# Dense attention scores as two 64-row matmuls, issued for two key blocks at a time

## The chip, the cores and the metric

The kernel runs on all 8 cores of one Trainium2 chip, two sequences of the batch on each core, with nothing exchanged between them. The metric is the device time of the slowest core, in microseconds (us). Some executions fall into a slower state in which the four cores of one die, sometimes of both, show a lower granted TensorE clock (0.816 on one die against 0.991 on the other in the changed kernel's run of 4770 us; 0.924 to 0.921 and 0.919 to 0.914 on both in one of 4394 us in experiment 6).

## The reference, cut to what matters

```python
x = x + 0.5 * swiglu(rmsnorm(x), gate1, up1, down1)
h = rmsnorm(x)
q_A, k_A, v_A, q_B, k_B, v_B, gates = split(h @ w_in)
# A: dense differential attention: 8 heads, each with two score maps (head dimension 64)
p = softmax(q_A @ k_A.T * 64**-0.5 - slope * |distance|)      # (head, 2, query, key)
o_A = rmsnorm((p[0] - lam * p[1]) @ v_A)                      # value dimension 128
# B: windowed attention: 16 heads of dimension 64, |distance| <= 128, with a sink
x = x + (sig(g_A) * (o_A @ P_A) + sig(g_B) * (o_B @ P_B)) @ w_out
x = x + 0.5 * swiglu(rmsnorm(x), gate2, up2, down2)
```

Both attentions contract over 64 elements for their scores, half of the 128 rows that TensorE's full matmuls have in the profile ("128*128"). The dense one has two score maps per head, so two contractions over 64 belong together.

## The kernel before: the parts that matter

The attention of a sequence is a list of steps. A dense step covers one block of 128 keys and a block of 384 (or 256) queries. It makes scores for both maps (QK) on TensorE (PE in the profile), takes exp on ScalarE (ACT), multiplies by a table of position biases on VectorE (DVE), and, LAG steps later, multiplies with the values (AV) on TensorE. When a block of queries is done, its AV sums are copied out of their PSUM banks, scaled, normalised and transposed in parts spread over the next steps; this is the evacuation. The two stretches of the run in which attention is at work, one for each sequence, are the attention phases. The steps are interleaved with matmuls of the feed-forward and projection stages ("fill"), so that TensorE has work while ACT and DVE are busy. A yielded number is a cost in TensorE columns, by which the fill is metered out.

```python
def attention(self, sq):
    # ... steps: per head 96 dense ("D"), then 16 windowed ("S")
    for i in range(n + LAG + 14):
        due = [f for (d, f) in self.later if d <= i]
        self.later = [x for x in self.later if x[0] > i]
        for f in due:
            yield f()                       # later parts of an evacuation
        if i < n:
            yield self.b_qk(i, steps[i])
        if LAG <= i < n + LAG:              # LAG = 3
            yield from self.b_av(i, steps[i - LAG], sq)

def b_qk(self, i, st):
    s = self.pslot()                        # one of two score slots, two PSUM banks each
    er, et = self.er[i % 2], self.et[i % NET]   # NET = 6
    # ...
    for c in range(2):
        ps = slice(64 * c, 64 * c + 64)
        if kind == "D":                     # kz[:, c] holds map c's keys, and zeros in the other half
            self.mm(self.bk[2 * s + c][:, 0:W], self.kz[:, c, k0:k0 + 128], self.q[0][:, q0:q0 + W], ...)
        else:                               # 64 rows of the array for each map
            self.mm(self.bk[2 * s + c][:, 0:W], self.k1[ps, k0:k0 + 128], self.q[1][ps, q0:q0 + W], ...)
    self.act(er[:, :, 0:W], <both banks of slot s>, AF.Exp, ..., scale=0.125)
    self.tt(et[:, :, 0:W], er[:, :, 0:W], tab, ALU.mult, ...)
    return 2 * W if kind == "D" else W + 400
```

A dense map's keys stand in one half of the rows with zeros in the other, so that the matmul has the full form (128*128 in the profile, 0.162 us from start to start at 384 columns) and there is no switch of tiling, which cost the windowed steps of before 0.094 us in and 0.103 us out. `load_D` loads a head's keys, queries, values and bias table when the head before has ended.

The softmax here doesn't subtract the row's maximum and nothing guards it: scores larger than these inputs give would overflow.

## Time and profile before

| | before |
|---|---|
| median of 5 runs, two of them slow | 4217.02 us (fast ones: 4207.8, 4216.3, 4217.0) |
| profiled run, slowest core | 4206.8 us |
| TensorE (PE) busy | 97% |
| attention phases, slowest core | 1170 and 1179 us |
| matmuls | 27872 in the program, the same number after |

Matmul durations in the profile overlap: a 512-column one is 382 ns long, but the next starts 216 ns after it. What counts is the distance from one start to the next, which a timeline gives. The prediction shows the lines.

### The profile page before, as it was taken

What the parts mean: (1) busy time and instruction counts of PE and PEld (TensorE: products, weight loads), DVE (VectorE), ACT (ScalarE), POOL (GpSimd) and SP (SyncE); (2) the same over time, 40 slices, a digit from 0 to 9 for tenths busy, and PEclk for the clock granted to TensorE, in tenths of its full rate; (3) what the DMA queues carried; (4) which work ended last, traced back from release to release, by engine and by line L of the source; (5) the groups of instructions that cost most, each with busy time, mean ns of one, the idle gap of its engine ahead of it and who ended that gap; (6) DMA issues with size and microseconds to landing.
All of it is one profiled execution on the core that took longest, in us unless ns stands there. A gap on an engine that the chain in (4) does not pass through costs nothing.

```text
span 4206.8 us, 82560 instructions; the slowest of 8 cores (4178.8 to 4206.8 us)
## 1 busy us (share of the span) xinstructions
PE 4084.3 (97%) x28032; PEld 2276.0 (54%) x28032; DVE 2319.0 (55%) x4768; ACT 2111.7 (50%) x3814; POOL 177.2 (4%) x235
## 2 busy tenths in 40 slices
PE   7999999999999999999999999999999999999998
PEld 3445445555665566556565565566556444444443
DVE  4332352447766765766357766776776544343533
ACT  2111421257777777777367777776777312121211
POOL 1000000000000000000000000000000000000000
PEclk9999999999999999999999999999999999999999
DMA  7977776656565655656944423443343465555543
GB/s 172 186 189 207 238 222 198 215 157 173 141 165 154 167 139 152 172 157 156 245 143 151 143 96 121 154 138 103 125 135 123 142 221 168 195 177 186 189 150 132
DMA packets 220581, 693.93 MB, mean 165 GB/s; under 512 B 22256, under 2 KB 80880, under 8 KB 218096
## 3 DMA queue, kind: packets, MB, share of 16 engines
q1 hardware_dynamic: 212432, 634.11, 47.6%
q0 software_dynamic: 7744, 54.53, 8.4%
q8 instruction: 240, 3.93, 0.4%
q14 instruction: 165, 1.35, 0.1%
HBM read 614.27 MB, written 160.79 MB: 184 GB/s over the span
## 4 chain that ended last, share of the span: by engine, by line
PE 85%; DMA 7%; DVE 3%; ACT 2%; issue 2%; SPq 1%; DVEq 0%; ACTq 0%; POOL 0%; POOLq 0%
PE bank L306 84%; DMA td<-td_d 2%; ACT er L309 1%; SPq L330 1%; DMA rd<-s_d 1%; DVE et L312 1%; DMA s_win<-ra 1%; DMA rd<-w_d 1%; DMA R<-x 1%; DMA vd_d<-sv 1%; PE bank L941 1%; DMA ra<-s_win 0%; DMA x_d<-R 0%; DMA qd_d<-sq 0%; DVE R L315 0%
## 5 line engine op out<-in xcount | busy, mean ns | idle before, releaser
L306 PE MATMUL bank<-H,ra 128*128 128x512 bf16 x8320 | 2200.8, 382 | 25.8 <-DMA ra<-s_win 6.1
L309 ACT ACTIVATE er<-bank 128x768 bf16<-128x768 f32 (+1 forms) x1792 | 1323.5, 745 | 571.5 <-PE bank L306 426.3
L306 PEld LDWEIGHTS bank<-H,ra 128*128 128x128 bf16 x8320 | 796.1, 99 | 772.5 <-issue 114.4
L312 DVE TENSOR_TENSOR et<-er,td 128x768 bf16<-128x768 bf16 (+1 forms) x1536 | 780.0, 512 | 637.3 <-ACT er L309 604.5
L306 PE MATMUL bank<-aT,rd 128*128 128x512 bf16 x2816 | 753.6, 382 | 15.2 <-DMA rd<-s_d 8.2
L306 PEld LDWEIGHTS bank<-vD,et 128*128 128x128 bf16 x8192 | 593.0, 98 | 286.0 <-issue 25.5
L306 PE MATMUL bank<-vD,et 128*128 128x129 bf16 x8192 | 723.2, 221 | 15.3 <-DVE obs L312 5.5
L306 PE MATMUL bank<-q,kz 128*128 128x384 bf16 (+1 forms) x3072 | 697.7, 309 | 10.7 <-ACT er L309 6.9
L315 DVE SCALAR_TENSOR_TENSOR fr<-fr,bank 128x512 f32<-128x512 f32 x480 | 329.4, 686 | 435.0 <-ACT fr L309 334.9
L309 ACT ACTIVATE fr<-bank 128x512 f32<-128x512 f32 x352 | 209.5, 595 | 665.0 <-PE bank L306 664.8
L306 PEld LDWEIGHTS bank<-q,kz 128*128 128x128 bf16 x3072 | 291.6, 98 | 261.3 <-issue 39.4
L306 PEld LDWEIGHTS bank<-aT,rd 128*128 128x128 bf16 x2816 | 267.4, 98 | 257.3 <-issue 40.1
L315 DVE SCALAR_TENSOR_TENSOR R<-bank,R 128x512 f32<-128x512 f32 x192 | 132.2, 688 | 301.1 <-PE bank L306 301.0
L312 DVE TENSOR_TENSOR aT<-fr,bank 128x512 bf16<-128x512 f32 x352 | 240.8, 684 | 71.3 <-PE bank L306 68.8
L309 ACT ACTIVATE fr<-bank,bgh 128x512 f32<-128x512 f32 x128 | 87.7, 686 | 291.3 <-PE bank L306 290.9
L309 ACT ACTIVATE ntmp<-R 128x512 f32<-128x512 f32 x224 | 135.5, 625 | 156.2 <-DVE R L315 109.0
L312 DVE TENSOR_TENSOR nacc<-nacc,ntmp 128x512 f32<-128x512 f32 x224 | 153.9, 687 | 62.1 <-ACT ntmp L309 59.9
L312 POOL TENSOR_TENSOR rs<-ms,mhalf 128x3 f32<-128x3 f32 (+1 forms) x96 | 88.1, 917 | 2181.9 <-DVE ms L321 2181.9
L312 DVE TENSOR_TENSOR et<-er,sw 128x768 bf16<-128x768 bf16 (+1 forms) x256 | 135.5, 538 | 65.8 <-ACT er L309 63.9
L306 PE MATMUL bank<-ra,H 128*128 128x256 bf16 x1280 | 169.3, 273 | 1.4 <-ACT sv L309 1.3
L327 DVE CAST sq<-bank 128x512 bf16<-128x512 f32 x104 | 71.5, 688 | 159.2 <-PE bank L306 113.7
L309 ACT ACTIVATE sq<-bank 128x512 bf16<-128x512 f32 x104 | 61.8, 596 | 187.4 <-PE bank L306 135.3
(84 smaller groups left out, 2360.5 us busy)
## 6 DMA issues: line engine op xcount, KB each, us to landing
ra<-s_gu SPq DMA_DIRECT2D x308, 512.0 KB, 4.4
rd<-s_d SPq DMA_DIRECT2D x112, 704.0 KB, 4.3
ra<-s_win SPq DMA_DIRECT2D x116, 512.0 KB, 5.7
ra<-s_pg SPq DMA_DIRECT2D x64, 512.0 KB, 3.7
ra<-s_pp SPq DMA_DIRECT2D x64, 512.0 KB, 3.4
R<-x SPq DMA_DIRECT2D x32, 512.0 KB, 7.8
x_d<-R SPq DMA_DIRECT2D x32, 512.0 KB, 6.2
R<-x_d SPq DMA_DIRECT2D x32, 512.0 KB, 6.6
```

What stands on the lines that cost most here:

```text
L306: self.S.add("pe", lambda e: e.matmul(out, lhsT=lhsT, rhs=rhs, start=start, stop=stop), r=r, w=w)
L309: self.S.add("act", lambda e: e.activation(out=out, in_=in_, func=func, **kw), r=r, w=w)
L312: self.S.add(eng, lambda e: e.tensor_tensor(out=out, in0=a, in1=b, op=op), r=r, w=w)
L315: self.S.add("dve", lambda e: e.scalar_tensor_tensor(out=out, in0=a, scalar=s, in1=b, op0=op0, op1=op1), r=r, w=w)
L327: self.S.add(eng, lambda e: e.tensor_copy(out=out, in_=in_), r=r, w=w)
L330: self.S.add(eng, lambda e: e.dma_start(out=out, in_=in_), r=r, w=w, dma=sem)
L941: self.S.add("pe", lambda e, q=q: e.transpose(out=bt[:, q * 128:(q + 1) * 128], in_=src[:, q, :], identity=self.ident), r=[sk, "ident"], w ...
```

## The change

Its intent is to make use of both halves of the array: the two maps' QK become two 64-row matmuls that run side by side, as the windowed ones of before do (starts 0.003 us apart in the median of its trace). As each switch of tiling costs time (0.094 us in and 0.103 us out, by the prediction's reading of the trace before), two steps are issued together, so that four matmuls share one entry and one exit. The windowed steps, tiled already, are paired too. The lag grows to 4 steps and there are more buffers. Queries and bias table are loaded in two parts, the first one earlier. Casting later weights to bf16 is tied to attention steps. The pacing constants are new. The later parts of an evacuation are now issued after a step's scores and AV, and no longer ahead of them. The core of the diff, with cuts marked:

```diff
-LAG = 3
-NET = 6
+QT = 14
+LAG = 4
+NET = 8
+QK2 = {384: 1375, 256: 1130}
...
-        self.kz = sb("kz", [128, 2, SEQ], BF16)
+        self.k0 = sb("k0", [128, SEQ], BF16)
...
-            if i < n:
-                yield self.b_qk(i, steps[i])
+            if i % 2 == 0 and i < n:
+                yield self.b_qk(i, steps[i:i + 2], sq)
...
+        for kind, u, bi, kc in sts:
...
+            s = self.pslot()
+            todo.append((s, W, tab, tk))
+            for c in range(2):
+                ps = slice(64 * c, 64 * c + 64)
+                self.mm(self.bk[2 * s + c][:, 0:W], k[ps, kc * 128:(kc + 1) * 128], q[ps, q0:q0 + W], True, True,
                         qk, [("bk", 2 * s + c)])
...
+        for n, (s, W, tab, tk) in enumerate(todo):
...  (exp and product of each step, as before)
+        if kind == "D" and bi == 5 and kc == 0 and u < 7:
+            self.load_D(sq, u + 1, 0, self.dma)
+        if kind == "D" and self.ahead and (bi < 4 and kc == 2 or bi == 2 and kc == 10):
+            self.precast(self.ahead.pop(0))
+        return QK2[W] + (720 if kind == "S" else 0)
...
-                    self.load_D(sq, u + 1, self.dma)
+                    self.load_D(sq, u + 1, 1, self.dma)
```

More of the change, by code (lines that the diff above doesn't have):

```diff
@@ L238, in decl_chip @@
         self.obf = sb("obf", [128, 3, 128], BF16)
-        self.obs = [sb("obs%d" % i, [128, 3, 128], BF16) for i in range(3)]
+        self.obs = [sb("obs%d" % i, [128, 3, 128], BF16) for i in range(4)]
         self.obn = 0
@@ L265, in decl_chip @@
         assert b0 + 39424 + NFF * TB * 2 <= self.ptr
-        self.ALIAS = (["q0", "q1", "k0a", "k0b", "kz", "k1", "k1b", "vD", "vS", "td0", "td1", "sw"] + ["er%d" % i for i in range(2)] +
+        self.ALIAS = (["q0a", "q0b", "q1", "k0", "k1", "k1b", "vD", "vS", "td0", "td1", "sw"] + ["er%d" % i for i in range(2)] +
                       ["et%d" % i for i in range(NET)])
@@ L278, in decl_chip @@
         self.drip = []
-        self.casting = False
     def bank(self, hold=False):
@@ L355, in init_rings @@
                       [("gu2", f) for f in range(22)] + [("d2", c) for c in range(8)])
-        self.nis = 0
     def issue(self, k, after=()):
@@ L361, in issue @@
             self.drip.pop(0)()
-        if self.ahead and self.casting:
-            self.nis += 1
-            if self.nis % 3 == 0:
-                self.precast(self.ahead.pop(0))
     def flush(self):
@@ L471, in setup2 @@
                 yield
-            if h == 7:
-                for j in range(2):
-                    S.add("dve", lambda e, j=j: e.memset(self.kz[64 - 64 * j:128 - 64 * j, j, :], 0.0), w=["kz", "dd"] + al)
             self.dma(self.td_d[h], self.tst[h % 2], [("tst", h % 2, j) for j in range(4)] + al, [("tdd", h)], ("c", 6 + h % 2))
@@ L653, in st_W @@
             if i == 8 and b % 4 == 3:
-                self.load_D(b // 4, 0, self.slow)
+                self.load_D(b // 4, 0, 0, self.slow)
+                self.load_D(b // 4, 0, 1, self.slow)
             if i == 1 and b == 7:
@@ L762, in st_O, with load_D @@
             self.issue("a")
-    def load_D(self, sq, h, dma):
-        c = slice(sq * SEQ, (sq + 1) * SEQ)
+    def load_D(self, sq, h, part, dma):
+        c0 = sq * SEQ
         bl = range(4 * sq, 4 * sq + 4)
-        for j in range(2):
-            dma(self.kz[64 * j:64 * j + 64, j, :], self.kd_d[h * 128 + 64 * j:h * 128 + 64 * j + 64, c],
-                [("kd", h // 2, b) for b in bl], ["k0" + "ab"[j]], ("bkz", j))
-        dma(self.q[0], self.qd_d[h * 128:(h + 1) * 128, c], [("qd", h // 2, b) for b in bl], ["q0"], ("bq", 0))
-        dma(self.vD, self.vd_d[sq, h], [("vd", sq, h // 2, b) for b in bl], ["vD"], ("bv", 0))
-        for j in range(2):
-            n = slice(NM // 2 * j, NM // 2 * (j + 1))
-            dma(self.td[:, n], self.td_d[h][:, n], [("tdd", h)], ["td%d" % j], ("btd", j))
+        n = slice(0, QT * 128) if part == 0 else slice(QT * 128, SEQ)
+        m = slice(0, QT * 128) if part == 0 else slice(QT * 128, NM)
+        r = slice(h * 128, (h + 1) * 128)
+        if part == 1:
+            dma(self.k0, self.kd_d[r, c0:c0 + SEQ], [("kd", h // 2, b) for b in bl], ["k0"], ("bk", 0))
+        dma(self.q[0][:, n], self.qd_d[r, c0 + n.start:c0 + n.stop], [("qd", h // 2, b) for b in bl],
+            ["q0" + "ab"[part]], ("bq0", part))
+        if part == 1:
+            dma(self.vD, self.vd_d[sq, h], [("vd", sq, h // 2, b) for b in bl], ["vD"], ("bv", 0))
+        dma(self.td[:, m], self.td_d[h][:, m], [("tdd", h)], ["td%d" % part], ("btd", part))
     def load_S(self, sq, p, dma):
@@ L797, in attention @@
         self.load_S(sq, 0, self.slow)
-        for i in range(n + LAG + 14):
-            due = [f for (d, f) in self.later if d <= i]
-            self.later = [x for x in self.later if x[0] > i]
-            for f in due:
-                yield f()
-            if i < n:
-                yield self.b_qk(i, steps[i])
+        for i in range(n + LAG + 15):
+            if i % 2 == 0 and i < n:
+                yield self.b_qk(i, steps[i:i + 2], sq)
             if LAG <= i < n + LAG:
                 yield from self.b_av(i, steps[i - LAG], sq)
+            for f in self.due(i):
+                yield f()
@@ L807, in attention @@
         assert not self.later
-    def b_qk(self, i, st):
-        kind, u, bi, kc = st
-        s = self.pslot()
-        er, et = self.er[i % 2], self.et[i % NET]
-        if kind == "D":
-            t0, nq = QBLOCKS[bi]
-            q0, W, sl = t0 * 128, nq * 128, 0
-            m0 = q0 - kc * 128 + 1920
-            tab = self.td[:, m0:m0 + W].unsqueeze(1).broadcast_to([128, 2, W])
-            tk, qk = ["td0", "td1"], ["q0", "k0a", "k0b", "kz"]
-        else:
-            lo, hi = max(0, kc - 1), min(15, kc + 1)
-            q0, W, sl = lo * 128, (hi - lo + 1) * 128, 1
-            off = (lo - kc + 1) * 128
-            tab = self.sw[:, :, off:off + W]
-            tk, qk = ["sw"], ["q1", "k1", "k1b"]
-        k0 = kc * 128
-        for c in range(2):
-            ps = slice(64 * c, 64 * c + 64)
-            if kind == "D":
-                self.mm(self.bk[2 * s + c][:, 0:W], self.kz[:, c, k0:k0 + 128], self.q[0][:, q0:q0 + W], True, True,
-                        qk, [("bk", 2 * s + c)])
-            else:
-                self.mm(self.bk[2 * s + c][:, 0:W], self.k1[ps, k0:k0 + 128], self.q[1][ps, q0:q0 + W], True, True,
-                        qk, [("bk", 2 * s + c)])
-        self.act(er[:, :, 0:W], self.ps[s].rearrange("p (c w) -> p c w", c=2)[:, :, 0:W], AF.Exp,
-                 [("bk", 2 * s), ("bk", 2 * s + 1)], ["er%d" % (i % 2)], scale=0.125)
-        self.tt(et[:, :, 0:W], er[:, :, 0:W], tab, ALU.mult, ["er%d" % (i % 2)] + tk, ["et%d" % (i % NET)])
-        return 2 * W if kind == "D" else W + 400
@@ new lines, in due, with b_qk @@
+    def due(self, i):
+        now = [f for (d, f) in self.later if d <= i]
+        self.later = [x for x in self.later if x[0] > i]
+        return now
+    def b_qk(self, i, sts, sq):
+        todo = []
+        for kind, u, bi, kc in sts:
+            if kind == "D":
+                t0, nq = QBLOCKS[bi]
+                q0, W = t0 * 128, nq * 128
+                m0 = q0 - kc * 128 + 1920
+                tab = self.td[:, m0:m0 + W].unsqueeze(1).broadcast_to([128, 2, W])
+                tk = ["td0"] * (m0 < QT * 128) + ["td1"] * (m0 + W > QT * 128)
+                q, k, qk = self.q[0], self.k0, ["q0a" if t0 < QT else "q0b", "k0"]
+            else:
+                lo, hi = max(0, kc - 1), min(15, kc + 1)
+                q0, W = lo * 128, (hi - lo + 1) * 128
+                off = (lo - kc + 1) * 128
+                tab = self.sw[:, :, off:off + W]
+                tk, q, k, qk = ["sw"], self.q[1], self.k1, ["q1", "k1", "k1b"]
+            s = self.pslot()
[3 more added lines that the diff above has]
+                self.mm(self.bk[2 * s + c][:, 0:W], k[ps, kc * 128:(kc + 1) * 128], q[ps, q0:q0 + W], True, True,
+                        qk, [("bk", 2 * s + c)])
+        for n, (s, W, tab, tk) in enumerate(todo):
+            x, y = (i + n) % 2, (i + n) % NET
+            er, et = self.er[x], self.et[y]
+            self.act(er[:, :, 0:W], self.ps[s].rearrange("p (c w) -> p c w", c=2)[:, :, 0:W], AF.Exp,
+                     [("bk", 2 * s), ("bk", 2 * s + 1)], ["er%d" % x], scale=0.125)
+            self.tt(et[:, :, 0:W], er[:, :, 0:W], tab, ALU.mult, ["er%d" % x] + tk, ["et%d" % y])
+        kind, u, bi, kc = sts[0]
+        if kind == "D" and bi == 5 and kc == 0 and u < 7:
[3 more added lines that the diff above has]
+        return QK2[W] + (720 if kind == "S" else 0)
@@ L920, in evac_D @@
         self.later += [(i + 1, f1), (i + 3, f1b), (i + 4, f2), (i + 6, f3), (i + 7, f3b), (i + 9, f4),
-                       (i + 13, lambda: self.tposes(self.obf, "obf", 0, t0, nq, self.od_d, "od", sq, u, bi == 5))]
+                       ((i + 14) & ~1, lambda: self.tposes(self.obf, "obf", 0, t0, nq, self.od_d, "od", sq, u, bi == 5))]
     def evac_S(self, i, sq, u, gi, bank):
@@ L925, in evac_S @@
         self.obn += 1
-        oi = self.obn % 3
+        oi = self.obn % 4
         obs, ok = self.obs[oi], ("obs", oi)
@@ L933, in evac_S @@
                 self.rn[:, 0:ng, :].unsqueeze(3).broadcast_to([128, ng, 2, 64]), ALU.mult, [("bk", bank), "rn"], [ok])
-        self.later += [(i + 6, lambda: self.tposes(obs, ok, 1, g0, ng, self.os_d, "os", sq, u, gi == 5))]
+        self.later += [((i + 7) & ~1, lambda: self.tposes(obs, ok, 1, g0, ng, self.os_d, "os", sq, u, gi == 5))]
     def tposes(self, src, sk, oi, t0, nq, dst, nm, sq, u, last):
@@ L970 @@
     COST = {"GU": NFF * 16 * TB, "D": 8 * NFF * TB, "W": 18 * 16 * TB, "P": 8 * 32 * TB, "O": 64 * TB}
-    BCOST = 8 * 16 * (4 * (768 + 810) + 2 * (512 + 540)) + 8 * 16 * (784 + 440) + 56 * GAP + 5000
+    BCOST = 64 * (4 * (QK2[384] + 1620) + 2 * (QK2[256] + 1080) + QK2[384] + 880 + 720) + 56 * GAP + 20000
     def build(self):
@@ L1006, in build @@
                 if si == s0:
-                    self.casting = True
                     self.gset = [6, 7]
```

## The prediction

> **What bounds the kernel now.** I read the spans of the cores first (4178.8 to 4206.8 us, granted clock 0.989 to 0.994: no core is throttled), then the page, the PE groups by form, and the timeline of a few microseconds.
>
> ```profile
> PE 4084.3 (97%) x28032; PEld 2276.0 (54%) x28032; DVE 2319.0 (55%) x4768; ACT 2111.7 (50%) x3814; POOL 177.2 (4%) x235
> ```
>
> PE looks full, but its ends are modelled, so I checked by the starts. The timeline has these lines in dense attention, where QK is "q,kz" (one head half zero-padded to all 128 rows):
>
> ```profile
> 1060.21 0.59 PE L306 MATMUL bank<-H,ra 128*128 128x512 bf16 x2
> 1060.64 0.49 PE L306 MATMUL bank<-q,kz 128*128 128x384 bf16 x2
> 1060.96 0.38 PE L306 MATMUL bank<-H,ra 128*128 128x512 bf16 x1
> 1061.18 0.51 PE L306 MATMUL bank<-vD,et 128*128 128x129 bf16 x6
> 1061.52 0.38 PE L306 MATMUL bank<-H,ra 128*128 128x512 bf16 x1
> ```
>
> Read only the first column. 0.43 us for two 512-wide matmuls: 0.216 each. Two padded 384-wide ones: 0.32, that is 0.162 each. Six 129-wide ones: 0.34, 0.057 each. Medians over all starts in the trace are the same, and a 256-wide one takes 0.109. PE streams without a hole. Giving every pair of neighbouring kinds its median distance, attention phase one (864 to 2035 us) needs 1112 of its 1170 us, phase two (2113 to 3292) 1148 of 1179. So only 58 + 31 = 89 us of both phases are stalls; the rest is matmul issue. A change pays by shortening what PE streams.
>
> The windowed attention already uses the form that the change brings, two 64-row matmuls in the two halves of the array:
>
> ```profile
> 1001.12 0.38 PE L306 MATMUL bank<-H,ra 128*128 128x512 bf16 x1
> 1001.43 0.34 PE L306 MATMUL bank<-q,k 64*128 64x384 bf16 x2
> 1001.70 0.60 PE L306 MATMUL bank<-H,ra 128*128 128x512 bf16 x2
> ```
>
> The matmul ahead now takes 0.310 instead of 0.216 (entry: +0.094). The two 64-row ones start 0.003 to 0.006 apart (call it 0.004). The next full one starts 0.265 after the second for 384 columns, 0.212 for 256: streaming 0.162 or 0.109, plus 0.103 of exit. One such step costs 0.094 + 0.004 + 0.265 = 0.363 us, against 2 x 0.162 = 0.324 padded. Tiling a single step loses; that is why before pads in the dense part.
>
> The counts, from the PE groups by form:
>
> ```profile
> L306 PE MATMUL bank<-q,kz 128*128 128x384 bf16 x2048 | 502.5, 327 | 4.0 <-ACT er L309 2.1 <-issue 0.2
> L306 PE MATMUL bank<-q,kz 128*128 128x256 bf16 x1024 | 195.2, 272 | 6.7 <-ACT er L309 4.8 <-ACT ot L309 0.3
> ...
> L306 PE MATMUL bank<-q,k 64*128 64x384 bf16 x448 | 75.5, 333 | 3.7 <-ACT er L309 2.8
> ...
> L306 PE MATMUL bank<-q,k 64*128 64x256 bf16 x64 | 9.1, 278 | 0.6 <-ACT ot L309 0.5
> ```
>
> [...] In the trace, full-array loads do overlap with full-array matmuls (98 ns each, nothing added to 0.216). For 64 rows before has no second load into a half that is still streaming, so no line of it tests this, and the change hangs on it. [...]
>
> **The change, part by part.**
>
> 1. Dense QK becomes 64-row, and two steps go together, so that four matmuls share one entry and one exit. Per four: 0.094 + 0.004 + X + 0.004 + exit, with X the distance from the first step's second matmul to the second step's first, in the same half. If its weight load is hidden, X = 0.162 (0.109 for 256). [...] The new pacing constants decide me. Pacing counts columns at 0.422 ns (old dense QK: 768 for 0.324 us). The constants 1375 and 1130 are then 0.580 and 0.477 us; my middle case gives 0.582 and 0.476. I take it that they were fitted to a run.
>  Dense: before 2048 x 0.162 + 1024 x 0.109 = 443 us. After 512 x 0.582 + 256 x 0.476 = 420. Gain 23. The 256-wide pairs lose (0.476 against 0.436); the 384-wide ones win (0.582 against 0.648).
> 2. Windowed QK is paired too: before 224 x 0.363 + 32 x 0.310 = 91 us; after 96 pairs of 0.582 and 32 mixed ones near 0.53 = 73. Gain 18.
> 3. No K padding: one 128-partition load per head in place of two halves with the same bytes; a memset goes. Nothing on PE.
> 4. q and the bias table are loaded in two parts, the first during the last query block. DVE waited 23.2 us for the table six times, but PE showed only 4.6 us behind DVE's product and 8.9 us for all holes over 1 us ahead of AV. I allow 5 us.
> 5. LAG 4, NET 8, four obs buffers: needed by the pairing, no time.
> 6. Weight precasts go from every third weight issue to fixed attention steps, so 10 of 50 move to phase two (DMA share 0.39 there, 0.59 in phase one). Nothing, or 2 us of the G-to-G holes.
>  The instruction order of the built kernel confirms it: the same 27872 matmuls, 896 runs of four 64-row ones, 875 of them right after a full matmul of other work, and some 4 to 6 full matmuls (512-column equivalents) between dense pairs.
>
> PE sum: 23 + 18 = 41 us off, all of it on the path that sets the end, since PE is that path.
>
> **Rivals.**
>
> A. ACT takes back part of it. A pair asks for both score slots at once: exp 0 and exp 1 of the previous pair must both be done.
>
> ```profile
> L309 ACT ACTIVATE er<-bank 128x768 bf16<-128x768 f32 x1248 | 1004.6, 810 | 447.7 <-PE bank L306 345.8 <-DVE et L312 58.1 <-DVE t L315 9.2
> ```
>
> (Groups by form, both phases.) In before I measured, for each QK, the time since the exp two steps earlier ended: median 1.14 and 1.18 us, tenth percentile 0.48 and 0.62. In pairs the later exp ends 0.81 later while its QK starts only 0.22 later, so some 0.6 us of slack is lost. Summing the shortfall below 0.6 over one QK in two gives 13 + 11 = 24 us. Against it: windowed pairs get more filler (+720 columns), and the tails of the evacuation now come after the pair's exps. I take 17 us. A burst of ACT work (three 0.39 us scalings, three squares at 0.49 with their read-outs) could double it.
>
> B. [...] 512 x 0.632 + 256 x 0.526 = 458, so dense QK loses 15, windowed gains 12: no gain, and with A 15 to 20 us slower, near 4230.
>
> C. X is hidden: 512 x 0.529 + 256 x 0.423 = 379 and 66 for windowed, 89 us off; less A, some 4140.
>
> D. Loads or clock: DMA share is at most 0.59 in the phases, and the clock is 0.99 already; neither speaks.
>
> **Range and chances.** The three fast runs before have 4207.8, 4216.3 and 4217.0. From 4214: -41 + 17 - 5 = -29, hence 4186 us. B and C give the range 4143 to 4227. Faster by over 2% (under 4130) needs C with hardly any stalls: 6%. Slower by over 2% needs stalls of over 120 us, beyond all 89 of before: 3%.
>
> **What would show it.** In the timeline after, pairs as four 64-row matmuls with 0.58 us from the first to the next full one less entry, i.e. 0.49 (0.38 for 256). X reads straight off: 0.215. The PE starts in both phases should need some 40 us less, and the holes ahead of QK, now 28 us, should be near 45, released by exp. If X is 0.265 or 0.162, step 1 is wrong; if QK holes exceed 70, my slack estimate is. If time outside the two phases moves by over 10 us, something that I dismissed (parts 3, 4, 6) matters.

It gave X, in part 1, two more values. One is 0.265 (0.212 for 256 columns), the distance that the trace before has from the last 64-row start to the next full matmul; rival B counts with it. The other is the middle case, 0.215 (0.162): streaming and 0.053 more for the weight load, an estimate of mine that no trace shows. The sum uses the middle case: a pair of 0.094 + 0.004 + 0.215 + 0.004 + 0.265 = 0.582 (0.476), hence 23 us for dense QK, 41 with the windowed steps, and 4186 us in the end.

## The result, and the profile after

The changed kernel takes 4136.45 us (median of 10 runs, lowest 4129.42); before takes 4217.02 (median of 17, lowest 4206.84); these medians include slow runs. The ratio of fast runs is 0.9813, with a 95% interval of 0.9799 to 0.9826: some 79 us faster. A ratio here is the mean time of one kernel's fast runs over that of the other's of the same rounds, so not quite the ratio of the medians. The predicted 4186 us missed; the predicted range reached down to 4143 only.

First the cores, by die, before and then after:

```profile
die 0 (median of its cores): 4195.8 us, clock 0.992
die 1 (median of its cores): 4193.7 us, clock 0.993
```

```profile
die 0 (median of its cores): 4123.4 us, clock 0.991
die 1 (median of its cores): 4114.3 us, clock 0.994
```

Both dies gained alike (72 and 79 us), single cores between 53 and 92, and the clock did not change. The busy line of the page after, and PE's two QK groups by form (count, busy us, mean ns of one, idle time before and what ended it):

```profile
PE 4003.5 (97%) x28032; PEld 2029.7 (49%) x28032; DVE 2327.7 (56%) x4766; ACT 2056.9 (50%) x3814; POOL 171.9 (4%) x237
```

```profile
L307 PE MATMUL bank<-q,k 64*128 64x384 bf16 x2496 | 329.0, 329 | 17.6 <-ACT er L310 10.5 <-ACT ot L310 2.4 <-DVE ms L322 0.8
...
L307 PE MATMUL bank<-q,k 64*128 64x256 bf16 x1088 | 114.7, 275 | 4.5 <-ACT er L310 2.5 <-ACT ot L310 1.0
```

PE's share is still 97%, and each QK matmul lasts as long as the windowed ones did before (329 against 333 ns). Neither says anything of the gain; their overlap does. The busy union of QK is 444 us, where the four QK groups of before had 782. The timeline of PE alone (start, length, what, count), and one line of the full timeline of the same core, with the weight loads (PEld):

```profile
1059.77 0.60 PE L307 MATMUL bank<-H,ra 128*128 128x512 bf16 x2
1060.30 0.50 PE L307 MATMUL bank<-q,k 64*128 64x384 bf16 x4
1060.73 0.60 PE L307 MATMUL bank<-H,ra 128*128 128x512 bf16 x2
1061.17 0.33 PE L307 MATMUL bank<-vD,et 128*128 128x129 bf16 x3
```

```profile
1060.29 0.11 PEld L307 LDWEIGHTS bank<-q,k 64*128 64x128 bf16 x4 [0.42 <-issue]
```

Four score matmuls fit between 1060.30 and 1060.73: 0.43 us, where four padded ones took 4 x 0.162 = 0.65. With an entry of 0.096 a pair costs 0.528. The medians over the trace (8 cores, 4642 pairs of 384 columns after a full matmul of other work; 1998 of 256):

| distance | predicted, 384 / 256 | measured median | measured mean |
|---|---|---|---|
| entry | 0.094 / 0.094 | 0.096 / 0.096 | 0.108 / 0.101 |
| step 1 to step 2 in the same half, X | 0.215 / 0.162 | 0.170 / 0.117 | 0.205 / 0.149 |
| last 64-row start to the next matmul of other work | 0.265 / 0.212 | 0.255 / 0.202 | 0.264 / 0.220 |
| the pair, entry included | 0.582 / 0.476 | 0.528 / 0.421 | 0.584 / 0.477 |

The means contain waits. Those of the last two rows take in 8 and 24 pairs with a small matmul of another kind behind them; without these the pair's means are 0.582 and 0.467.

X is streaming (0.162, 0.109) and 0.008 us more, and the way out is 0.093 beyond streaming, where it was 0.103 behind a single step in the trace before. The second step's weight load is hidden, and the line with the loads shows it: all four were done by 1060.41, while the first step's matmuls streamed until the second step's started at 1060.47. Over the trace, the second step's load into a half starts 11 ns (median) after the first step's matmul in that half, and has ended 66 ns before its own matmul starts.

To see where all the time went I gave each pair of neighbouring matmul kinds one undisturbed distance, called what is above it a stall, and took the mean of all eight cores of the profiled runs. (The prediction used core 1's own medians, hence its smaller 89 us of stalls.)

| us, mean of 8 cores | before | after | difference |
|---|---|---|---|
| QK issue, entries and exits included | 532 | 442 | -90 |
| stalls in the phases | 116 | 122 | +7 |
| - of these ahead of QK | 41 | 49 | +8 |
| - ahead of the dense AV | 27 | 11 | -16 |
| - ahead of transposes | 10 | 16 | +6 |
| stalls outside the phases | 75 | 83 | +8 |
| fill, inside and outside | 2849 | 2849 | 0 |

The sum is -75 us, as is the mean of the cores' spans (4194 to 4119). The phases got 96 us shorter, the rest 21 longer, but 12 of these are fill that moved out of the phases, presumably by the new pacing.

### The profile page after: what moved, and what is told of

The parts are those of the page before. It is cut to its first block, busy times and chain, and to the rows that moved or that the text cites. A ratio compares the mean times of both kernels' runs of the same rounds, so it can differ in the third digit from the quotient of the medians.

```text
span 4131.4 us, 81948 instructions; the slowest of 8 cores (4108.7 to 4131.4 us)
## 1 busy us (share of the span) xinstructions
PE 4003.5 (97%) x28032; PEld 2029.7 (49%) x28032; DVE 2327.7 (56%) x4766; ACT 2056.9 (50%) x3814; POOL 171.9 (4%) x237
## 4 chain that ended last, share of the span: by engine, by line
PE 82%; DMA 6%; DVE 4%; ACT 4%; issue 3%; SPq 1%; POOL 0%; DVEq 0%; ACTq 0%; POOLq 0%
PE bank L307 81%; ACT er L310 2%; DVE et L313 1%; DMA ra<-s_win 1%; DMA rd<-s_d 1%; SPq L331 1%; DMA rd<-w_d 1%; DMA td<-td_d 1%; DMA s_win<-ra 1%; DMA R<-x 1%; PE bank L945 1%; DMA vd_d<-sv 1%; DMA ra<-s_gu 0%; DMA qd_d<-sq 0%; ACT ntmp L310 0%
## 5 line engine op out<-in xcount | busy, mean ns | idle before, releaser
L307 PE MATMUL bank<-H,ra 128*128 128x512 bf16 x8320 | 2124.5, 383 | 21.6 <-DMA ra<-s_win 13.8
L310 ACT ACTIVATE er<-bank 128x768 bf16<-128x768 f32 (+1 forms) x1792 | 1239.4, 744 | 497.2 <-PE bank L307 366.6
L307 PEld LDWEIGHTS bank<-H,ra 128*128 128x128 bf16 x8320 | 760.5, 99 | 860.9 <-issue 226.0
L307 PE MATMUL bank<-aT,rd 128*128 128x512 bf16 x2816 | 718.7, 382 | 14.6 <-DMA rd<-w_d 7.4
L307 PE MATMUL bank<-q,k 64*128 64x384 bf16 (+1 forms) x3584 | 438.6, 312 | 22.1 <-ACT er L310 13.0
L307 PEld LDWEIGHTS bank<-aT,rd 128*128 128x128 bf16 x2816 | 253.8, 98 | 294.7 <-issue 80.1
L307 PEld LDWEIGHTS bank<-q,k 64*128 64x128 bf16 x3584 | 122.3, 94 | 328.0 <-issue 323.7
```

The source lines that it names most:

```text
L307: self.S.add("pe", lambda e: e.matmul(out, lhsT=lhsT, rhs=rhs, start=start, stop=stop), r=r, w=w)
L310: self.S.add("act", lambda e: e.activation(out=out, in_=in_, func=func, **kw), r=r, w=w)
```

## The experiments

My theory once the result was known: the gain is QK's issue time, because the weight load of the second step is hidden; entry and exit make it pay only with two steps together. The rivals: 64-row matmuls are cheaper however they stand (1); the lag, its buffers or the pairing alone carry the gain (2); the halves of the array have their own queues (3); the earlier loads carry it (4). Beside each run the kernel before ran on the same chip.

### 1. Tiling without pairing

Edit, on the kernel before:

```diff
-            dma(self.kz[64 * j:64 * j + 64, j, :], self.kd_d[...])
+            dma(self.kz[64 * j:64 * j + 64, 0, :], self.kd_d[...])
-                self.mm(..., self.kz[:, c, k0:k0 + 128], self.q[0][:, q0:q0 + W], ...)
+                self.mm(..., self.kz[ps, 0, k0:k0 + 128], self.q[0][ps, q0:q0 + W], ...)
```

> The kernel before, dense QK as two 64-row matmuls of one step, no pairing, nothing else changed. Theory 1 (the gain is QK issue time, and entry and exit must be shared by two steps): each dense step costs entry 0.096 + 0.003 + exit 0.255 = 0.354 us (384) or 0.301 (256) against 0.324 and 0.218 padded: 1024 x 0.030 + 512 x 0.083 = 73 us slower than before, 55 to 90 allowed. Rival 1 (64-row matmuls are cheaper however they stand): faster than before by 20 us or more.

Measured: 4289.4 and 4310.4 us (fast), against a mean of 4222.6 for before: 77 us slower. Its timeline:

```profile
1061.08 0.34 PE L306 MATMUL bank<-q,kz 64*128 64x384 bf16 x2
1061.35 0.39 PE L306 MATMUL bank<-H,ra 128*128 128x512 bf16 x1
1061.58 0.50 PE L306 MATMUL bank<-vD,et 128*128 128x129 bf16 x6
```

The full matmul starts 0.27 us after the pair of 64-row ones. The way out alone, streaming included, takes 0.265 of the 0.324 us that two padded matmuls take, and 0.1 of entry comes on top, so single tiled steps lose, as the sum said. The first rival falls.

### 2. The same pairing, with and without tiling

To have room for the padded keys, both kernels use LAG 3, seven product buffers and three output buffers.

```diff
 control, on the changed kernel:          padded, on the control:
-LAG = 4                                  -k[ps, kc * 128:(kc + 1) * 128], q[ps, q0:q0 + W]
-NET = 8                                  +self.kz[:, c, kc * 128:(kc + 1) * 128], q[:, q0:q0 + W]
+LAG = 3                                  (dense steps only; kz is loaded and zeroed as in before)
+NET = 7
-... for i in range(4)]   # obs
+... for i in range(3)]
```

> The changed kernel with LAG 3, seven et buffers and three obs buffers (it is the control for the next run, which needs the room). Theory 1: 60 to 80 us faster than before, at most 15 us behind the changed kernel. Rival 2 (the gain is fewer stalls, from the longer lag and the added buffers): less than 40 us faster than before.

> The LAG 3 control with dense QK zero-padded to 128 rows again, pairing, split loads, precasts and pacing constants kept. Theory 1: dense QK returns to 443 us of issue from 377, so 66 us slower than the LAG 3 control (50 to 80), within 25 us of before. Rival 2 (pairing, lag, loads or precasts carry the gain): within 20 us of the LAG 3 control.

Both gave wrong results (relative error 0.060). That was not intended: with three output buffers a windowed result was overwritten before its transpose. The times were 4194.2 us twice for the control, ratio 0.9932 (0.9886 to 0.9977), and 4241.25 in the one fast run of the padded kernel. I mended both, with the windowed transposes two steps earlier, and ran them again.

> The LAG 3 control with the fault mended (with three obs buffers the windowed transposes are issued two steps earlier, before the buffer is used again). Right results, and the time of the faulty one, 0.993 of before, within 0.006.

> The mended LAG 3 control with dense QK zero-padded. The faulty pair differed by 47 us (one fast run), with issue 67 us longer and phase stalls 14 us shorter. So 40 to 60 us slower than the mended control, 4235 to 4255 us, no faster than before. If it comes within 20 us of the control, row tiling is not what carries the gain.

Right results: the control 4175.3 and 4179.6 us, ratio 0.993 (0.9905 to 0.9955); padded 4229.4 and 4232.2. With everything else equal, tiling is worth 53 us in dense attention at LAG 3. A padded kernel with LAG 4 was not run, so what tiling is worth there is not shown. The padded kernel's timeline shows what it replaces, four at 0.65 us in place of 0.43:

```profile
1059.95 0.81 PE L307 MATMUL bank<-q,kz 128*128 128x384 bf16 x4
1060.60 0.59 PE L307 MATMUL bank<-H,ra 128*128 128x512 bf16 x2
```

By the account above, its issue is 67 us longer (509 against 442), as the theory said, and its phase stalls are 14 us shorter (157 against 172). Paired and padded, the kernel is no faster than before (4230.8 against 4206.8 in the same rounds).

The control says something else too. It is 29 us faster than before, where the changed kernel is 79 faster. The account puts it on AV: 68 us of stalls ahead of it at LAG 3, 11 at LAG 4. PE's waits in the control (who waited for whom, us in total, times, longest) have this line, which has 0.3 us in the changed kernel:

```profile
PE bank L307 <- DVE pc L328: 30.0, 49, 1.6
```

"pc" is the copy that frees an AV bank at the end of a query block. It is 30 of the 57 us; another 10 are waits for the windowed result "obs" (13.2 us against 3.2), and the rest was not sorted. So part of the second rival seemed right: once steps are paired, LAG 4 is worth some 50 us. Two more runs ask what it is about the lag.

### 3. The lag: its length, or its parity

First LAG 4 in the kernel before:

```diff
-LAG = 3
-NET = 6
+LAG = 4
+NET = 7
```

> The kernel before with LAG 4 and seven et buffers, still padded and unpaired. Theory 1 (QK issue carries the gain; the longer lag only pays back what pairing takes): issue is unchanged, the AV stalls of the phases fall from 27 us towards the 12 of the changed kernel: 10 to 20 us faster than before. Rival 2 (the lag carries the gain): over 40 us faster.

Measured: 4224.6 to 4230.3 us, ratio 1.001 (0.9981 to 1.0039). My 10 to 20 us were wrong, and so were the rival's 40. AV stalls stayed (25 us), and QK stalls rose from 41 to 71. A longer lag carries nothing by itself.

Then LAG 5 in the changed kernel, with nine product buffers:

```diff
-LAG = 4
-NET = 8
+LAG = 5
+NET = 9
```

> The changed kernel with LAG 5 and nine product buffers. Parity theory: an odd lag puts the end of a query block on the even step, so the copies that free the AV banks stand on DVE behind the two products whose exps have only just been issued, as at LAG 3; AV stalls go back to 40 to 70 us and the kernel is 30 to 60 us slower than with LAG 4. Length theory (a longer lag covers the later scores of a pair): AV stalls stay at 11 us or less, and the time is within 8 us of LAG 4 or better.

Measured: 4168.9 and 4171.8 us, ratio 0.9911 (0.9882 to 0.9939), so 41 us slower than LAG 4 by the ratios, 36 by the times (of other rounds). The profiled run was a slow one, so I read a core of its undisturbed die (clock 0.993); the mean AV stall of that die is 52 us:

```profile
PE bank L307 <- DVE pc L328: 21.7, 45, 2.1
```

Of the two theories it is the parity. The reason is read from the order of the instructions, and the line above covers 22 of the 52 us only. Pairs are issued at even steps, and a query block ends at a key block of odd number plus LAG. With LAG 3 or 5 this is an even step. The copy then stands on DVE behind the products of a pair whose exps have only just been asked for, and the next AV waits for its bank. With LAG 4 the block ends on an odd step, which issues no scores. In the kernel before every step issues scores ahead of its AV, so LAG 4 changes nothing there; this would also be why AV's stalls fell from 27 to 11 us with the change, but that is argued from the order of the instructions and not tried.

### 4. One load per head

```diff
-            self.load_D(sq, u + 1, 0, self.dma)        # at the last query block
...
+                    self.load_D(sq, u + 1, 0, self.dma)   # at the head's end
                     self.load_D(sq, u + 1, 1, self.dma)
```

> The changed kernel with both parts of q and of the bias table loaded at the head's end, as before. Theory 1: 0 to 8 us slower than the changed kernel, all of it in stalls ahead of AV and QK at the first steps of each head. Rival 4 (the gain is earlier loads): over 25 us slower.

Measured: 4147.0 and 4148.3 us, 0.982 of the before of its rounds (4220.3 and 4226.8). The phases took 7 us more than in the changed kernel, 6 of these ahead of the windowed AV. Rival 4 falls; the split loads are worth a few microseconds.

### 5. Another order of the four matmuls

```diff
-            for c in range(2):         # step by step: half 0, half 1, half 0, half 1
+        for c in range(2):             # half by half: half 0, half 0, half 1, half 1
+            for s, W, tab, tk, kc, q, k, qk, q0 in todo:
```

> The changed kernel with the four matmuls in the order half 0 step 0, half 0 step 1, half 1 step 0, half 1 step 1. Theory 1 with starts in order: the third cannot start before the second, so the four take 0.17 us (384) or 0.117 (256) more: 624 x 0.17 + 272 x 0.117 = 138 us slower than the changed kernel (110 to 160), some 60 us slower than before. Rival 3 (each half has its own queue, a later matmul of a free half passes): within 15 us of the changed kernel.

Measured: 4183.6 to 4187.7 us, ratio 0.9912 (0.9878 to 0.9945), so 42 us slower than the changed kernel by the ratios, 52 by the times (its rounds ran on another chip, where before was slower too): neither number was right. The median from the first start to the next full matmul stayed 0.435 us for 384 columns (0.432 in the changed kernel); for 256 it rose to 0.351 (0.325). One such group of the trace, with its semaphore updates:

```
start us   operation              updates
1068.119   MATMUL 64x384          -
1068.125   MATMUL 64x384          score semaphore + 1
1068.292   MATMUL 64x384          -
1068.299   MATMUL 64x384          score semaphore + 1
```

In the program the updates stand on the third and fourth matmuls. So the one that started second is the third of the program: it is for the other half, and started 0.167 us ahead of the program's second, which is for the half of the first. Over the trace, 5645 groups have their updates on the second and fourth start like this one. Of the 1523 in which the second start comes over 0.1 us after the first, 1339 have them on the third and fourth, as in the program. Rival 3 is right that a later matmul of the free half passes; that each half has a queue of its own is not shown. Most of the lost time comes from somewhere else, from groups like this one of the timeline:

```profile
1061.72 0.33 PE L307 MATMUL bank<-q,k 64*128 64x384 bf16 x1
1062.22 0.50 PE L307 MATMUL bank<-q,k 64*128 64x384 bf16 x3 [0.17 <-ACT ot L310]
1062.65 0.60 PE L307 MATMUL bank<-H,ra 128*128 128x512 bf16 x2
```

The program's second matmul writes the second score slot, which was not free yet. In this group nothing passed the wait for it: half 1 of the first step, whose slot was free, started 0.5 us after half 0 (1062.22 against 1061.72), and so its exp was late too. The mean from first start to next full one is 0.533 against 0.479 for 384 columns and 0.410 against 0.371 for 256 (slowest cores). Over 624 and 272 pairs (mixed ones counted as 50 to 50) that is 44 us, of which some 9 are the risen medians and the rest waits.

### 6. What the remaining QK stalls wait for

In the changed kernel 33 us of QK's stalls are a wait for the second slot. I sorted them by what its exps had waited for: 15 us the bare chain (the first exp began 0.16 us after the modelled end of its own two matmuls), 12 us other ACT work ahead, 5 us DVE's product of two steps earlier, which still held the exp's result buffer. The chain in the timeline of the changed kernel:

```profile
1060.30 0.50 PE L307 MATMUL bank<-q,k 64*128 64x384 bf16 x4
...
1060.79 1.51 ACT L310 ACTIVATE er<-bank 128x768 bf16<-128x768 f32 x2
...
1062.60 0.50 PE L307 MATMUL bank<-q,k 64*128 64x384 bf16 x4
```

Two exps end at 1062.30, and the next pair starts at 1062.60: 0.3 us of room. Two runs take ACT work away. The first puts the three scalings of an evacuation on DVE, as one instruction; the second also the squares and their sums:

```diff
-            for q in range(nq):
-                self.act(self.t1[:, q, :], pcv[:, 0, q, 0:128], AF.Copy, ..., scale=self.rcp[:, 0, q:q + 1])
+            self.tt(self.t1[:, 0:nq, :], pcv[:, 0, :, 0:128], <rcp broadcast>, ALU.mult, ...)
```

> The changed kernel with the three scalings of each evacuation moved from ACT (1.0 to 1.2 us in one go) to one DVE instruction. If the 50 us of QK stall in the phases are ACT's exp coming late because of other ACT work, they fall by 10 to 25 us and the time by as much. Rival (the stall is the exp chain itself, PE to ACT to PE): no change within 5 us.

> As the run before, and the squares with their sums (1.5 us of ACT in one go) moved to two DVE instructions. If ACT bursts cause the QK stall: 15 to 40 us faster than the changed kernel. If DVE becomes the limit instead: AV stalls rise from 12 us and the time is the same or worse than with the scalings alone.

Measured: 4149.9 to 4189.8 us, ratio 0.9862 (0.974 to 0.9984, too wide to tell it from the changed kernel); and 4158.6 to 4163.3, ratio 0.9851 (0.9827 to 0.9875), slower than the changed kernel's 0.9813. In the first, slot waits behind other ACT work did not fall (12 us before, 15 in its trace). In the second, they fell from 12 us to 2, but those for DVE's product rose from 5 to 25 of now 41 us. Exp's waits for that product over the whole run, in the changed kernel, and then in the second of these:

```profile
ACT er L310 <- DVE et L313: 68.9, 99, 2.3
```

```profile
ACT er L310 <- DVE et L313: 189.3, 218, 3.2
```

The work had moved from one side of the exp to the other. If so, a third buffer for exp's results should help there. I ran it on both kernels, with the changed kernel as control:

```diff
-        self.er = [sb("er%d" % i, [128, 2, 384], BF16) for i in range(2)]
+        self.er = [sb("er%d" % i, [128, 2, 384], BF16) for i in range(3)]
-            x, y = (i + n) % 2, (i + n) % NET
+            x, y = (i + n) % 3, (i + n) % NET
```

> The changed kernel itself, as control on this chip: 0.981 of before, within its interval of 0.9799 to 0.9826.

> The changed kernel with three exp result buffers in place of two. In the trace after, some 5 of the 33 us of wait for the second score slot go to an exp held up by DVE's product two steps earlier, 15 to the bare chain of QK and two exps, 12 to other ACT work ahead of exp. So 3 to 8 us faster than the changed kernel. Rival (buffers are the cause): 15 us or more faster.

> Scalings and squares on DVE as in the run before that was slower, and three exp result buffers. There, ACT bursts had gone from the wait for the second slot (12 us to 2) but waits for DVE's product had risen from 5 to 25. If the third buffer covers those, 33 us of wait become about 17: 8 to 18 us faster than the changed kernel. Rival (DVE itself is late, whatever the buffers): as slow as the run with two buffers, 15 us behind the changed kernel.

Measured in these rounds: the changed kernel 4130.6 to 4135.5 us, ratio 0.9766 (0.9731 to 0.9801; below its earlier interval's 0.9799 only because before was slower on this chip, 4214 to 4248). Three buffers: 4121.6 and 4126.6 us, ratio 0.9745 (0.97 to 0.9789). Three buffers with the work on DVE: 4133.1 to 4144.3, ratio 0.9779 (0.9753 to 0.9806). Waits of exp for the product, three buffers alone, then with the work on DVE:

```profile
ACT er L310 <- DVE et L313: 29.0, 42, 2.6
```

```profile
ACT er L310 <- DVE et L313: 65.9, 90, 5.1
```

The third buffer takes most of that wait away in both, and by mean times makes the changed kernel 8.5 us faster, just above the 3 to 8 expected. But the waits for the second slot, from which the 3 to 8 were worked out, stayed at 34 us (33 in the control), so the gain, if it is one, has another cause, which was not looked for. The intervals overlap, so it is the best version by its two fast runs and not clearly so. It does not turn the DVE variant into a gain (6 us behind the control): 17 us of its waits for the second slot now come from the second of the two exps, which waits for DVE's product of three steps earlier. The third buffer moved that wait from the first exp to the second. Neither 8 to 18 us faster nor 15 slower came true.

### 7. Windowed steps singly

```diff
-            if i % 2 == 0 and i < n:
-                yield self.b_qk(i, steps[i:i + 2], sq)
+            if i < n and (i % 2 == 0 or steps[i][0] == "S"):
+                yield self.b_qk(i, steps[i:i + (2 if steps[i][0] == "D" else 1)], sq)
...
-        return QK2[W] + (720 if kind == "S" else 0)
+        return QK2[W] if kind == "D" else 1048     # two of these are a pair's 1375 + 720, rounded
```

> The changed kernel with the windowed steps (224 of 384, 32 of 256 columns) issued singly again. Theory 1: their issue returns from 66 to about 91 us, so 25 us slower than the changed kernel, 15 to 30 allowed. Rival (pairing the windowed steps is worth nothing, since their exps limit them): within 8 us.

Measured: ratio 0.9794 (0.9764 to 0.9824), 4144.9 us on average against 4132.6 for the changed kernel of the same rounds: 12 us slower, between theory and rival. Two of its windowed steps:

```profile
1275.95 0.34 PE L307 MATMUL bank<-q,k 64*128 64x384 bf16 x2
1276.22 0.60 PE L307 MATMUL bank<-aT,rd 128*128 128x512 bf16 x2
1276.76 0.34 PE L307 MATMUL bank<-q,k 64*128 64x384 bf16 x2
1277.03 0.39 PE L307 MATMUL bank<-aT,rd 128*128 128x512 bf16 x1
```

Issue is 23 us longer, as computed (465 against 442), but phase stalls are 12 us shorter (108 against 120). So half of this issue gain had been given back as waiting, where it was 14 of 67 us for the dense tiling.

## Why the prediction was wrong, point by point

- **What bounds the kernel: right.** PE's issue sets the end (its matmuls are 84% of the chain that ended last before, 81% after), and all of the gain came out of it.
- **Step 1, X: the step that failed.** The prediction had three values of X, and wrote "The new pacing constants decide me." and "my middle case gives 0.582 and 0.476. I take it that they were fitted to a run." X measured 0.170 (384) and 0.117 (256), which is Rival C's case but for 0.008. A pair issues in 0.528 and 0.421 us. The assumption that failed is that the second step's weight load is not hidden and puts X 0.053 us above streaming; that was my estimate, which no trace showed, and X is 0.008 above. (The 0.053 was no load's duration either: the loads have medians of 92 to 98 ns in the traces.) QK issue fell by 90 us, not 41: this one term was short by 49 us, and the miss was 50 (4136 against 4186). That the rest of the sum came out (12 us lost forecast, 15 measured in stalls) is in part luck: 16 us less ahead of the dense AV, for which it had no term, stood against more stalls ahead of transposes, ahead of other work and outside the phases.
- **Why the constants misled.** They are 0.580 and 0.477 us, near the measured means of a pair (0.584 and 0.477, or 0.582 and 0.467 with full matmuls behind), and these means contain the waits for the score slots. So the guess that they come from a run fits, but it is not shown. I set a mean with waits against padded distances without waits (0.162, 0.109), and then added the waits once more as Rival A.
- **Step 2, windowed pairing: mis-sized.** 18 us were predicted. The same X makes it 23 of issue by the run with single windowed steps, and 12 of time.
- **Rival A: there, but smaller.** Stalls ahead of QK grew by 8 us, not 17, and all stalls of the phases by 7. The term read ACT bursts as a main danger; moving them away showed that the chain of QK and two exps, and DVE on the other side, hold the slot as well.
- **Part 4, loads: about right in size.** 5 us allowed; the phases took 7 more without the split. But the stalls ahead of the dense AV were as low with one load, so that fall is not from the loads but, by the order of the instructions, from where the block's end falls.
- **Part 5, "LAG 4 ... no time": right for the kernel before (ratio 1.001), wrong for the paired one.** There an odd lag costs 36 to 49 us. This did not make the forecast wrong, as the change brought the even one, but the sum had no term for it.
- **Parts 3 and 6: not tried alone.** The prediction's own check failed here: the time outside the phases grew by 21 us, and its limit was 10. Of these, 12 are fill from inside the phases, for which the prediction had no part, and 8 are stalls, whose cause is open.
- **Rivals B, D: fell.** X was not 0.265, and the clock stayed at 0.99. Rival C came true in its mechanism; its time, "some 4140", was 4 us off, and my range, which ended at 4143, left out even that figure, as I had taken its chance to be small.

## What to carry to other kernels

Two 64-row matmuls side by side paid here when two steps shared one entry and one exit of the tiling (0.528 us a pair against 0.648 padded at 384 columns, 0.421 against 0.436 at 256); alone, a step of 384 columns lost against zero padding here (0.363 against 0.324). Work out such a choice from distances between starts, keep bare distances and means with waits apart, and when one unmeasured distance decides the sign or the size, give its other values the width of the range that they deserve. When an engine's issue gets shorter, expect part of it back as waits (14 of 67 and 12 of 23 us here), and check what the new order of issue puts ahead of each copy that frees a bank: one step of lag was worth 36 to 49 us here.
